# The first three weight pieces multiplied in quarters, as pairs of the first shift and scale come in

## The chip, the cores and the metric

The kernel runs on one core of one Trainium2 chip. The metric is the device time of one execution in microseconds (us). TensorE is PE in the profile, its weight loads PEld, VectorE is DVE, ScalarE is ACT, GpSimd is POOL, and SP is the engine that issues most transfers.

## What is computed

Two layers over 256 tokens of width 1024, in float32. Layer 0 mixes with a gated MLP, layer 1 with attention; each is followed by a mixture of experts (64 experts, 8 per token). Cut to the place that the change touches:

```
sh1, sc1, ... = split(silu(c) @ ada_w[0] + ada_b[0], 6)
h = rmsnorm(x, norm_mix[0]) * (1 + sc1) + sh1
z = gelu(h @ w_in + b_in)
u, v = split(z, 2)
v = layernorm(v);  sv = w_s @ v + b_s  (8 groups, chunks of 128 tokens)
x = x + g1 * ((u * sv) @ w_out)
x = x + g2 * moe(...)
```

The shift `sh1` and the scale `sc1` are 1024 values each, from a product of one row with a 1024 x 2048 part of `ada_w`.

## The kernel before

All weights come from memory in pieces of 1 MB (128 partitions x 2048 floats), called here by the tensors they are cut from: `wada` (the shifts, scales and gates, 24 pieces for a layer), `win` (16 pieces of `w_in`), `wout`, `wkva`, `wqkvo`, and three pieces for each expert. They land in a ring of 9 buffers with the tag "w" (`load`, L245); SP issues them in program order, and a piece whose buffer is still in use holds up those behind it.

A `wada` piece i gives 256 of the values. `Sum` in mode "p" (L312) multiplies it with 8 matmuls of 32x256 into a PSUM tile, ACT copies that back into the piece, and `total` (two matmuls with one column) adds up the four parts. `close` adds the bias on DVE. In mode "v" the multiplication is done on DVE, and one matmul pair does the rest. Piece 0 to 3 of layer 0 are the shift for feature tiles 0 to 7, two tiles each, and pieces 4 to 7 are the scale for the same tiles.

The way in, in the phase "pb": `wT` (the group weights) is masked on POOL; two matmuls add up its columns, 16 small ones make the bias rows `t2`; a loop over the 8 `wada` pieces multiplies each and totals it before the next is multiplied. In the second round of that loop `x` is normalised by the root of its mean square (`rstd_of`, `normed`) and transposed on PE (`transposed`) into four PSUM tiles. When all 8 totals stand, one addition and `scale_of` give shift and scale, and `feature_major_halves` writes the modulated h as two halves with fewer bits (`hT`: the rounded value, and what is left of it), for each of the 8 feature tiles an ACTIVATE on ACT, a CAST and a subtraction on DVE or, for the last three tiles, the subtraction on POOL.

The products with `w_in` follow as steps. The steps 0 to 15 are of class `Tok` (L476): a piece `win` i makes the steps 2i and 2i + 1, with 4 feature tiles each, for both token tiles: 24 matmuls of 128x256 a step (`mm3`: three products of the halves). Before its matmuls a step needs its weights as halves: `high` (a CAST on ACT, 128x1024) and `low` (a subtraction on DVE). `split` does `high` three steps ahead and `low` two steps ahead; there are 4 buffers for the halves (`scr`). Steps 16 to 31 (`Feat`) and then 16 of class `Out` follow. Between steps `tick` does the other `wada` and `wkva` pieces a few operations at a time (`BEGIN` says at which step each begins), and what has not begun by the end of the steps is done at the start of the expert phase by `rest` and `pump`.

`bvs` are four biases of 512 values spread over all partitions; the first is fetched by SP ahead of the steps, the others by ACT at the steps 2, 6 and 10. From the end of the way in, `pin` holds all engines to the program's order.

Of the kernel before, what the change touches and what calls it, by code (L numbers as in the profile page):

```python
# [8 lines left out]
F32 = mybir.dt.float32  # L9
# [4 lines left out]
ALU = mybir.AluOpType  # L14
# [16 lines left out]

LA = 3


ITEMS = [("a", i) for i in (16, 17, 18, 19, *range(8, 16), 20, 21, 22, 23)] + [("k", i) for i in range(8)]
# [142 lines left out]
def tile_model(ctx: ExitStack, tc: tile.TileContext, A: dict, out: bass.AP):  # L178
# [3 lines left out]
    class Ordered:  # L182


        def __init__(self, eng):
            self.eng = eng
# [33 lines left out]
    def h1(shape, dt=F32):  # L220
        return sb.tile(list(shape), dt, tag="h1", name=nm("h1"), bufs=5)
# [7 lines left out]
    def wk(shape=(P, 512), dt=F32):  # L229
        return ps.tile(list(shape), dt, tag="wk", name=nm("wk"), bufs=4)  # L230
# [176 lines left out]
    def pieces(x):  # L407

        return [x[:, q // 2, 512 * (q % 2):512 * (q % 2) + 512] for q in range(4)]
# [15 lines left out]
        G.tensor_tensor(r, ms, mhalf, ALU.pow)  # L425
        return r

    def normed(xs, rt, r):

        ro = pieces(rt)  # L430
        for q in (0, 2, 1, 3):
            if q < 2:
                V.tensor_scalar(ro[q], xs[q], r[:, 0:1], None, ALU.mult)
            else:
                S.activation(ro[q], xs[q], AF.Copy, scale=r[:, 1:2])

    def transposed(rt, tags=("wk",) * 4):

        o = []
        for c2 in range(KT // 2):  # L440
            pt = ps.tile([P, 2, 256], F32, tag=tags[c2], name=nm(tags[c2]), bufs=4)
            for cc in range(2):
                for tt in range(2):
                    c = 2 * c2 + cc
                    T.transpose(pt[:, cc, tt * P:(tt + 1) * P], rt[:, tt, c * P:(c + 1) * P], ident)
                o.append(pt[:, cc, :])
        return o

    def feature_major_halves(pts, mods, outs):

        for (hi, lo), (a, b) in zip(outs, mods):
            for c, pt in enumerate(pts):
                t = h1((P, 256))
                S.activation(t, pt, AF.Identity, bias=b[:, c:c + 1], scale=a[:, c:c + 1])
                V.tensor_copy(hi[:, c, :], t)
                (G if c > 4 else V).tensor_tensor(lo[:, c, :], t, hi[:, c, :], ALU.subtract)

    class Feat:

# [16 lines left out]
    class Tok:  # L476


        def __init__(self, w, kh, src, ep, prev=None, dst=None):
            self.w, self.kh, self.src, self.ep_, self.prev, self.p = w, kh, src, ep, prev, dst  # L480

        def part(self):
            return self.w[:, 4 * self.kh:4 * self.kh + 4, :]

        def mm(self):
            if self.p is None:
                self.p = self.prev.p if self.prev else [ac((P, 256)) for _ in range(2)]
            for tt in range(2):
                for k in range(4):
                    kk = 4 * self.kh + k  # L490
                    c = slice(tt * P, (tt + 1) * P)
                    mm3(self.p[tt], [self.src[0][:, kk, c], self.src[1][:, kk, c]],
                        [self.h[:, 0, k, :], self.h[:, 1, k, :]], kk == 0, kk == KT - 1)

        def ep(self):
            if self.kh:
# [649 lines left out]
    def phase(name):  # L1146
        return tc.tile_pool(name=name, bufs=1, reuse_waits="tile")


    with phase("pb") as pool:  # L1150
        lnb = wp.tile([2, 2048], F32, tag="w", name=nm("w"), bufs=9)
        nc.sync.dma_start(lnb, A["lnb"][:, 0:2048])
        lns = wp.tile([2, 1024], F32, tag="w", name=nm("w"), bufs=9)
# [1 line left out]
        hT = [pool.tile([P, KT, 256], F32R, tag="hh", name=nm("hh"), bufs=2) for _ in range(2)]  # L1155
        wT = pool.tile([P, 8, P], F32, tag="wT", name="wT")
        nc.sync.dma_start(wT, A["ws"].rearrange("s (g t) -> s g t", g=8))
        G.affine_select(wT, wT, [[0, 8], [1, P]], ALU.is_ge, 0.0, base=0, channel_multiplier=-1)
        t2 = b8((P, 16, P))


        for q in range(2):
            pr = wk((1, 512))
            T.matmul(pr, onesf[:, 0:1], wT[:, 4 * q:4 * q + 4, :].rearrange("s g t -> s (g t)"), start=True, stop=True)
            S.copy(lns[0:1, 512 * q:512 * q + 512], pr)
        for q in range(4):
            pt = wk((P, 4, P))
            for i in range(4):
                c = 4 * q + i
                g = c // 2  # L1170
                T.matmul(pt[:, i, :], lnb[:, c * P:(c + 1) * P], lns[:, g * P:(g + 1) * P], start=True, stop=True)
            S.copy(t2[:, 4 * q:4 * q + 4, :], pt)


        pa = wk((P, 16))
        for i in range(8):
            f = ada(0, i, load(A["wada"][0, i]), "p")
            if i == 1:
                nc.sync.dma_start(xt, A["x"].rearrange("(a p) d -> p a d", p=P))
            f.begin()  # L1180
            f.total(pa[:, 2 * i:2 * i + 2])
            if i == 1:
                rt = b8((P, 2, D))
                normed(pieces(xt), rt, rstd_of(pieces(xt), rt))
                pts = transposed(rt, ("acc",) * 4)


        wi = [None] * 16
        wo = [None] * 8
        first = []  # L1190

        def fetch(x):
# [8 lines left out]
            elif x[0] == "s":  # L1201
                first.append(expert(A["wsh"][0]))

        fetch(("i", 0))
        early = [high(wi[0][:, 4 * q:4 * q + 4, :], pool) for q in range(2)]
        for q in range(2):
            low(early[q], wi[0][:, 4 * q:4 * q + 4, :])
        V.tensor_tensor(adaT[0][:, 0:16], pa, pkc("adab0")[:, 0:16], ALU.add)
        scm = scale_of(adaT[0][:, 8:16], pkc("nmix0"), "scm0")
        feature_major_halves(pts, [(scm, adaT[0][:, 0:8])], [hT])  # L1210

        fetch(("i", 1))
        bvs = {}

        def fetch_bv(a, n):
            bvs[a] = s2((P, n))
            (S if pin else nc.sync).dma_start(bvs[a], A["bv"][:, a:a + n].to_broadcast([P, n]))

        fetch_bv(0, 512)
        nc.sync.dma_start(tab, A["tab"])  # L1220
        rw = router(0)
        weighing = weigh(0, rw)
        for x in QUEUE:
            fetch(x)
        pin.update(engines)

        uT = [b8() for _ in range(2)]
        v = [b8((P, 2048)) for _ in range(2)]
# [75 lines left out]
        steps[0].h, steps[1].h = early  # L1304
        steps += out_
        for k in range(2, LA):
            steps[k].h = high(steps[k].part(), pool)
        for k in range(n + 16):
            for at, x in BEGIN:
                if at == k:  # L1310
                    begin(x, lighter(k < 30))
            if k in (2, 6, 10):
# [12 lines left out]
            if 1 <= k <= n:  # L1325
                steps[k - 1].ep()
            if k % 4 == 1 and 1 < k < 18:
# [34 lines left out]
    with phase("pe") as pool:  # L1362
# [142 lines left out]
        ts = {}  # L1505
        for c in range(KT + 2):
            if c < KT:
                V.tensor_tensor(xT[c], pts[c], rb, ALU.mult)
# [139 lines left out]
```

## Time and profile before

| | us |
|---|---|
| median of 3 runs | 1416.7 (1415.97 to 1423.08) |
| the profiled execution, its own time | 1416.0 |
| its span, first to last instruction | 1414.2 |
| PE busy in the span | 1369.3 (97%) |
| DVE / ACT / POOL busy | 728.5 / 462.7 / 57.4 |

The profiled execution lasts 1.8 us longer than its span. Nearly every instruction of an engine carries the line L192 in the profile, that of the helper which records them, so groups are told apart by the names of the tiles. A float32 matmul is recorded as two, so that 8 of them stand as x16; those on halves (`scr`, `hh`) stand singly, and some records are missing. In a timeline a row is a run of equal instructions: its start, how long it lasts, the engine, out<-in, and in brackets the idle time ahead of it and what ended that. PEclk is the granted TensorE clock, 1.00 for 2.4 GHz and 0.50 for 1.2 GHz.

### The profile page before, as it was taken

The numbers are of one execution on the slowest core, as the hardware profiler recorded it, in microseconds if no ns is written. First come the engines' busy times: TensorE is split into PE (matmuls) and PEld (weight loads), VectorE is DVE, ScalarE is ACT, GpSimd is POOL, SyncE is SP. The second block draws the span as 40 slices with busy tenths as digits, with TensorE's granted clock in tenths as the row PEclk, the third lists the DMA queues.
The fourth block names the chain that finished last, engine by engine and source line by source line (L and its number), as shares of the span: only waits on it lengthen the run. The fifth ranks groups of instructions, "written<-read, shape, count | busy, mean of one in ns | idle before, by whom it ended". The sixth has DMA issues, their size and how long they took to land. (4 is left out here: it accounts for less than half of the span.)

```text
span 1414.2 us, 27956 instructions
## 1 busy us (share of the span) xinstructions
PE 1369.3 (97%) x11406; PEld 889.9 (63%) x11406; DVE 728.5 (52%) x1489; ACT 462.7 (33%) x958; POOL 57.4 (4%) x68
## 2 busy tenths in 40 slices
PE   7899999999999999999989999999999999999996
PEld 4799876745555555555548977775555555555553
DVE  0776655344444444444447866544444444444544
ACT  2544434212223222322234554422222222222222
POOL 0100002000000000000001121200000000000000
PEclk8899999999999999999999999999999999999999
DMA  9967776699999999999996867479999999999995
GB/s 371 366 271 304 281 248 248 229 366 425 425 426 426 425 426 425 423 426 426 426 416 277 317 242 268 173 277 396 410 426 425 426 426 425 426 424 425 426 426 217
DMA packets 72700, 516.66 MB, mean 365 GB/s; under 512 B 8308, under 2 KB 8436, under 8 KB 10358
## 3 DMA queue, kind: packets, MB, share of 16 engines
q1 hardware_dynamic: 72132, 514.03, 89.0%
q8 instruction: 91, 1.49, 0.4%
q10 hardware_dynamic: 436, 0.79, 0.2%
q14 instruction: 41, 0.34, 0.1%
HBM read 513.75 MB, written 1.05 MB: 364 GB/s over the span
## 5 line engine op out<-in xcount | busy, mean ns | idle before, releaser
L192 PE MATMUL wk<-w,b 128*32 128x256 f32 (+1 forms) x4928 | 406.6, 381 | 4.9 <-DMA w<-in_wexp_dram 4.9
L192 PEld LDWEIGHTS wk<-w,b 128*32 128x32 f32 (+1 forms) x4928 | 233.0, 121 | 144.2 <-DMA w<-in_wexp_dram 8.3
L192 DVE TENSOR_TENSOR s<-s,s 64x512 fp32r<-64x512 f32 x220 | 150.9, 686 | 125.3 <-ACT s L192 121.8
L192 PE MATMUL wk<-w,ht 128*32 128x512 f32 (+1 forms) x1232 | 212.5, 601 | 0.4 <-ACT ht L192 0.4
L192 DVE TENSOR_TENSOR s<-wk,g 128x512 f32<-128x512 f32 x110 | 76.1, 692 | 184.4 <-PE wk L192 184.4
L192 PE MATMUL wk<-s,b 128*128 128x256 f32 (+2 forms) x1024 | 149.6, 295 | 0.0
L192 ACT CAST s<-s 64x512 fp32r<-64x512 f32 x220 | 134.3, 611 | 15.1 <-DVE s L192 12.4
L192 PEld LDWEIGHTS wk<-s,b 128*128 128x128 f32 (+1 forms) x1024 | 124.7, 185 | 15.7 <-DVE scr L192 0.7
L192 ACT COPY ht<-wk 128x128 f32<-128x128 f32 x110 | 29.3, 266 | 314.1 <-PE wk L192 314.1
L192 PE MATMUL acc<-s,h 128*128 128x512 f32 x440 | 131.6, 420 | 0.4 <-DVE s L192 0.2
L192 ACT ACTIVATE b<-wk,adaT,sc 128x256 f32<-128x256 f32 x112 | 63.3, 565 | 180.7 <-DVE b L192 180.7
L192 DVE TENSOR_SCALAR b<-wk,sc,adaT 128x256 f32<-128x256 f32 x112 | 61.0, 544 | 100.8 <-PE wk L192 100.6
L192 ACT CAST scr<-w 128x1024 fp32r<-128x1024 f32 x80 | 83.5, 1049 | 87.1 <-PE wk L192 39.1
L192 PEld LDWEIGHTS wk<-w,ht 128*32 128x32 f32 (+1 forms) x1232 | 50.4, 120 | 94.3 <-issue 91.1
L192 PEld LDWEIGHTS acc<-s,h 128*128 128x128 f32 x440 | 74.0, 188 | 52.7 <-DVE s L192 38.1
L192 ACT ACTIVATE h<-wk 64x256 f32<-64x256 f32 (+1 forms) x114 | 43.0, 377 | 187.3 <-PE wk L192 187.3
L192 DVE TENSOR_TENSOR scr<-w,scr 128x1024 fp32r<-128x1024 f32 x80 | 99.3, 1248 | 4.8 <-ACT scr L192 4.5
L192 DVE SCALAR_TENSOR_TENSOR h<-wk,ws,h 64x256 f32<-64x256 f32 x110 | 53.9, 490 | 67.6 <-ACT h L192 66.8
L192 PEld LDWEIGHTS wk<-ident,h 64*128 64x128 f32 (+1 forms) x226 | 22.5, 137 | 92.9 <-issue 84.4
L192 PE MATMUL wk<-hh,scr 128*128 128x256 f32 x576 | 73.8, 285 | 0.0
L192 PEld LDWEIGHTS wk<-hh,scr 128*128 128x128 f32 x576 | 70.2, 191 | 3.3 <-issue 3.3
L192 DVE SCALAR_TENSOR_TENSOR w<-w,cs 128x256 f32<-128x256 f32 x119 | 58.6, 493 | 2.9
(240 smaller groups left out, 1256.3 us busy)
## 6 DMA issues: line engine op xcount, KB each, us to landing
w<-in_wexp_dram SPq DMA_DIRECT2D x384, 1024.0 KB, 15.1
w<-in_wada_dram SPq DMA_DIRECT2D x48, 1024.0 KB, 7.0
w<-in_win_dram SPq DMA_DIRECT2D x16, 1024.0 KB, 8.9
w<-in_wqkvo_dram SPq DMA_DIRECT2D x16, 1024.0 KB, 7.6
w<-in_wout_dram SPq DMA_DIRECT2D x8, 1024.0 KB, 4.9
w<-in_wkva_dram SPq DMA_DIRECT2D x8, 1024.0 KB, 4.8
w<-in_wsh_dram SPq DMA_DIRECT2D x6, 1024.0 KB, 5.6
xt<-in_x_dram SPq DMA_DIRECT2D x1, 1024.0 KB, 9.9
```

The lines of the kernel that those rows point to most:

```text
L192: r = f(*a, **k)
```

## The change

The order of the way in is new, and `pin` holds the engines to the program's order from its first line on.

- `x` is loaded ahead of the `wada` pieces, and the pieces come in pairs: `wada` 0 and 4, `win` 0, `wada` 1 and 5, `win` 1, `wada` 2 and 6, `win` 2, `wada` 3 and 7.
- `x` is transposed as it is; the root is spread along the tokens by two matmuls (`along`), copied to `rb`, and multiplied in after the transpose, by four DVE operations of 128x512 into `xn`.
- `modulated(q)` totals one pair, closes both, makes two values of the scale, and writes the halves of two feature tiles, all on ACT and DVE.
- `Tok.mm` takes the feature tiles it is to do. `first_mm(i, q)` multiplies a quarter of piece i (two feature tiles, 12 matmuls). Both token tiles of these three pieces share one PSUM tile (`joint`), so that three pieces need three.
- A list written out by hand mixes these with the multiplications of the pairs, `high` and `low`. The step loop begins at step 6, no longer at 0.
- The first two `bvs` are fetched by ACT, one behind the other, in the middle of that list. `BEGIN` starts at step 6 too, no longer at 4, so 20 of the other pieces begin within the steps, no longer 21.

```diff
-MAIN = [("i", i) for i in range(2, 16)] + [("o", i) for i in range(8)]
+MAIN = [("i", i) for i in range(PRE, 16)] + [("o", i) for i in range(8)]
...
-BEGIN = [(4 + 2 * i, x) for i, x in enumerate(ITEMS) if 4 + 2 * i < 46]
+BEGIN = [(2 * PRE + 2 * i, x) for i, x in enumerate(ITEMS) if 2 * PRE + 2 * i < 46]
...
-        pa = wk((P, 16))
-        for i in range(8):
-            f = ada(0, i, load(A["wada"][0, i]), "p")
...
-            f.begin()
-            f.total(pa[:, 2 * i:2 * i + 2])
...
+        def modulated(q):
+
+            pt = wk((P, 4))
+            for j, i in enumerate((q, 4 + q)):
+                fs[i].total(pt[:, 2 * j:2 * j + 2])
+            for j, i in enumerate((q, 4 + q)):
+                fs[i].close(pt[:, 2 * j:2 * j + 2])
+            c = slice(2 * q, 2 * q + 2)
+            V.scalar_tensor_tensor(scm[:, c], adaT[0][:, 8 + 2 * q:10 + 2 * q], 1.0, pkc("nmix0")[:, c], ALU.add, ALU.mult)
+            for k in (2 * q, 2 * q + 1):
+                t = h1((P, 256))
+                S.activation(t, pieces(xn)[q][:, 256 * (k % 2):256 * (k % 2) + 256], AF.Identity, bias=adaT[0][:, k:k + 1],
+                             scale=scm[:, k:k + 1])
+                V.tensor_copy(hT[0][:, k, :], t)
+                V.tensor_tensor(hT[1][:, k, :], t, hT[0][:, k, :], ALU.subtract)
...
+        modulated(0)
+        half(0)
+        bias_rows(3)
+        multiply(1)
+        first_mm(0, 0)
+        multiply(5)
+        modulated(1)
+        first_mm(0, 1)
+        half(2)
+        multiply(2)
+        half(1)
+        first_mm(1, 0)
+        first_mm(1, 1)
+        multiply(6)
+        modulated(2)
+        half(4)
+        half(3)
+        fetch_bv(0, 512)
+        fetch_bv(512, 512)
+        first_mm(0, 2)
+        first_mm(1, 2)
+        first_mm(2, 0)
+        multiply(3)
+        first_mm(2, 1)
+        half(5)
+        multiply(7)
+        first_mm(2, 2)
+        modulated(3)
+        k = 2 * PRE
+        half(k)
+        for i in range(PRE):
+            first_mm(i, 3)
+            if i:
+                steps[2 * i - 1].ep()
...
+        for k in range(k, n + 16):
```

The order on PE, at the first products with `w_in`. `w` are pieces, `scr` the halves of a `win` piece, `hh_106` and `hh_107` the two halves of h. Before, the totals of the last pieces (`c_76,w`) stand right ahead of them:

```order
L192 MATMUL wk_270<-w_268,cs 32x256 x8
L192 MATMUL wk_142<-c_76,w_268 128x1 x2
L192 MATMUL wk_284<-w_282,cs 32x256 x8
L192 MATMUL wk_142<-c_76,w_282 128x1 x2
L192 MATMUL acc_457<-scr_298,hh_106 128x256 x2
L192 MATMUL acc_457<-scr_298,hh_107 128x256
```

With the change (`w_111` and `w_113` are `wada` 0 and 4, `w_117` is `wada` 1, `w_104,w_102` make bias rows):

```order
L194 MATMUL wk_208<-w_113,cs 32x256 x8
L194 MATMUL wk_218<-w_104,w_102 128x128 x4
L194 MATMUL wk_332<-c_76,w_111 128x1 x2
L194 MATMUL wk_332<-c_76,w_113 128x1 x2
L194 MATMUL wk_351<-w_104,w_102 128x128 x4
L194 MATMUL wk_357<-w_117,cs 32x256 x8
L194 MATMUL acc_367<-scr_348,hh_106 128x256 x2
L194 MATMUL acc_367<-scr_348,hh_107 128x256
```

The first quarter now stands behind the totals of one pair and the multiplication of `wada` 1, and five more multiplications stand behind it.

The order on SP, at the first pieces. Before:

```order
L249 DMA w_143<-in_wada_dram 128x2048
L249 DMA w_157<-in_wada_dram 128x2048
L1179 DMA xt<-in_x_dram 128x2x1024
L249 DMA w_212<-in_wada_dram 128x2048
L249 DMA w_226<-in_wada_dram 128x2048
```

With the change:

```order
L1145 DMA xt<-in_x_dram 128x2x1024
L251 DMA w_111<-in_wada_dram 128x2048
L251 DMA w_113<-in_wada_dram 128x2048
L251 DMA w_115<-in_win_dram 128x2048
L251 DMA w_117<-in_wada_dram 128x2048
L251 DMA w_119<-in_wada_dram 128x2048
```

`x` goes ahead of two pieces, and `win` 0 is now the fourth transfer of 1 MB instead of the tenth.

The order on ACT behind the third pair (`h_109`, `h_110` are its modulated tiles, `scr_485` and `scr_554` halves of `win` 2, `w_129` and `w_131` are `wada` 3 and 7). With the change:

```order
L194 ACTIVATE h_109_477<-b_19_141,adaT_96,scm_224 128x256
L194 ACTIVATE h_110_481<-b_19_141,adaT_96,scm_224 128x256
L194 CAST scr_485<-w_127 128x1024
L194 CAST scr_488<-w_121 128x1024
L194 DMA s_113_491<-in_bv_dram 128x512
L194 DMA s_114_493<-in_bv_dram 128x512
L194 COPY w_129<-wk_532 128x256
L194 CAST scr_554<-w_127 128x1024
L194 COPY w_131<-wk_557 128x256
```

Before, no transfer stood on ACT ahead of a copy that the shift waits for. In the built program the first of the two waits until `wada` 3 has landed, the second until `win` 3 has.

## Rows read from the trace of the kernel before

**Rows 1.** The page, 40 slices of the span: granted clock and DMA share, tenths.

```profile
PEclk8899999999999999999999999999999999999999
DMA  9967776699999999999996867479999999999995
```

**Rows 2.** Busy time by stretch: stretch, length, busy us (instructions), clock, DMA share, GB/s.

```profile
13.00:26.00 13.00, 12.02 (x72) 7.39 (x75) 2.99 (x9) 4.06 (x10) 0.70 (x1) 0.50 1.01 425
...
27.00:36.00 9.00, 6.57 (x80) 3.89 (x80) 0.00 (x0) 1.86 (x5) 0.00 (x0) 1.00 0.92 351
37.00:46.00 9.00, 4.94 (x27) 3.61 (x20) 5.61 (x15) 6.27 (x12) 0.00 (x0) 0.50 1.01 425
44.00:46.00 2.00, 2.00 (x10) 2.00 (x11) 2.00 (x6) 2.00 (x5) 0.00 (x0) 0.50 1.04 430
...
60.00:200.00 140.00, 140.00 (x1151) 125.66 (x1150) 94.28 (x170) 61.15 (x101) 1.82 (x2) 1.00 0.76 282
...
240.00:245.00 5.00, 4.47 (x51) 2.34 (x51) 4.63 (x10) 3.38 (x7) 5.00 (x5) 0.66 0.36 115
...
310.00:340.00 30.00, 30.00 (x282) 16.98 (x280) 14.12 (x29) 7.63 (x17) 0.00 (x0) 1.00 1.01 423
```

**Rows 3.** Timeline of PE on the way in.

```profile
9.70 4.48 PE L192 MATMUL wk<-w,w 2*128 2x128 f32 x32
...
17.48 1.93 PE L192 MATMUL wk<-w,cs 128*32 128x256 f32 x16
...
22.37 3.25 PE L192 MATMUL acc<-ident,b 128*128 128x128 f32 x14
...
29.56 0.61 PE L192 MATMUL wk<-c,w 128*128 128x1 f32 x4 [0.48 <-ACT w L192]
30.09 1.07 PE L192 MATMUL wk<-w,cs 128*32 128x256 f32 x16
...
38.64 1.01 PE L192 MATMUL wk<-c,w 128*128 128x1 f32 x4 [0.47 <-ACT w L192]
...
43.83 5.72 PE L192 MATMUL acc<-scr,hh 128*128 128x256 f32 x34 [0.68 <-DVE scr L192]
50.58 16.20 PE L192 MATMUL acc<-scr,hh 128*128 128x256 f32 x133 [1.04 <-POOL hh L192]
66.72 1.07 PE L192 MATMUL wk<-w,cs 128*32 128x256 f32 x16
```

**Rows 4.** Timeline of all engines, from the last total to the first half of h.

```profile
39.69 0.17 DVE L192 TENSOR_TENSOR adaT<-wk,pk 128x16 f32<-128x16 f32 x1 [20.23 <-PE wk L192]
39.90 0.17 DVE L192 SCALAR_TENSOR_TENSOR scm<-adaT,pk 128x8 f32<-128x8 f32 x1
40.10 1.48 ACT L192 ACTIVATE h<-acc,adaT,scm 128x256 f32<-128x256 f32 x3 [1.51 <-DVE scm L192]
40.70 0.29 DVE L192 CAST hh<-h 128x256 fp32r<-128x256 f32 x1 [0.63 <-ACT h L192]
...
41.03 0.43 DVE L192 TENSOR_TENSOR hh<-h,hh 128x256 fp32r<-128x256 f32 x1
```

**Rows 5.** Timeline of ACT: `high` of two steps, each released by a step's end.

```profile
61.11 1.05 ACT L192 CAST scr<-w 128x1024 fp32r<-128x1024 f32 x1 [1.20 <-issue]
...
64.00 1.05 ACT L192 CAST scr<-w 128x1024 fp32r<-128x1024 f32 x1 [1.84 <-PE acc L192]
```

**Rows 6.** Groups of DVE from 60 to 66 us: `low`; busy us, mean ns of one.

```profile
L192 DVE TENSOR_TENSOR scr<-w,scr 128x1024 fp32r<-128x1024 f32 x3 | 3.7, 1219 | 0.0
```

**Rows 7.** Timeline of DVE: the first use of `x`, released by its landing.

```profile
12.91 1.29 DVE L192 BATCH_NORM_STATS2 st<-xt 128x6 f32<-128x512 f32 x2 [11.15 <-DMA xt<-in_x_dram]
```

**Rows 8.** Timeline of PE after the steps and at the start of the experts.

```profile
231.45 0.66 PE L192 MATMUL wk<-ident,t 128*128 128x128 f32 x4
...
240.88 4.48 PE L192 MATMUL wk<-w,cs 128*32 128x256 f32 x48
```

**Rows 9.** Timeline of SP's queue: the first expert pieces chosen by the routing.

```profile
242.03 19.82 SPq L249 DMA_DIRECT2D w<-in_wexp_dram  x6
```

More of the change, by code (lines that the diff above doesn't have):

```diff
@@ L445, in transposed @@
                     T.transpose(pt[:, cc, tt * P:(tt + 1) * P], rt[:, tt, c * P:(c + 1) * P], ident)
-                o.append(pt[:, cc, :])
+            o.append(pt)
         return o
[L449 to L456, printed above, removed]
     class Feat:
@@ L476, in tile_model, with __init__, mm @@
     class Tok:
-        def __init__(self, w, kh, src, ep, prev=None, dst=None):
-            self.w, self.kh, self.src, self.ep_, self.prev, self.p = w, kh, src, ep, prev, dst
+        def __init__(self, w, kh, src, ep, prev=None):
+            self.w, self.kh, self.src, self.ep_, self.prev, self.p = w, kh, src, ep, prev, None
+            self.joint = False
         def part(self):
             return self.w[:, 4 * self.kh:4 * self.kh + 4, :]
-        def mm(self):
+        def mm(self, ks=range(4)):
             if self.p is None:
@@ L488, in mm @@
             for tt in range(2):
-                for k in range(4):
+                for k in ks:
                     kk = 4 * self.kh + k
@@ L492, in mm @@
                     mm3(self.p[tt], [self.src[0][:, kk, c], self.src[1][:, kk, c]],
-                        [self.h[:, 0, k, :], self.h[:, 1, k, :]], kk == 0, kk == KT - 1)
+                        [self.h[:, 0, k, :], self.h[:, 1, k, :]], kk == 0 and not (self.joint and tt), kk == KT - 1)
         def ep(self):
@@ L1157, in tile_model, with bias_rows @@
         nc.sync.dma_start(wT, A["ws"].rearrange("s (g t) -> s g t", g=8))
+        nc.sync.dma_start(xt, A["x"].rearrange("(a p) d -> p a d", p=P))
+        wi = [None] * 16
+        wo = [None] * 8
+        wa = {}
+        for q in range(4):
+            for i in (q, 4 + q):
+                wa[i] = load(A["wada"][0, i])
+            if q < PRE:
+                wi[q] = load(A["win"][q])
         G.affine_select(wT, wT, [[0, 8], [1, P]], ALU.is_ge, 0.0, base=0, channel_multiplier=-1)
         t2 = b8((P, 16, P))
[L1162 to L1166, printed above, removed]
+        def bias_rows(q):
             pt = wk((P, 4, P))
@@ L1172, in tile_model, with multiply @@
             S.copy(t2[:, 4 * q:4 * q + 4, :], pt)
-        pa = wk((P, 16))
-        for i in range(8):
-            f = ada(0, i, load(A["wada"][0, i]), "p")
-            if i == 1:
-                nc.sync.dma_start(xt, A["x"].rearrange("(a p) d -> p a d", p=P))
-            f.begin()
-            f.total(pa[:, 2 * i:2 * i + 2])
[L1182 to L1189, printed above, removed]
+        for q in range(2):
+            pr = wk((1, 512))
+            T.matmul(pr, onesf[:, 0:1], wT[:, 4 * q:4 * q + 4, :].rearrange("s g t -> s (g t)"), start=True, stop=True)
+            S.copy(lns[0:1, 512 * q:512 * q + 512], pr)
+        xn = b8((P, 2, D))
+        r = rstd_of(pieces(xt), xn)
+        pts = transposed(xt, ("acc",) * 4)
+        fs = {}
+        def multiply(i):
+            fs[i] = ada(0, i, wa[i], "p")
+            fs[i].begin()
+        bias_rows(0)
+        multiply(0)
+        bias_rows(1)
+        pr = along([r[:, tt:tt + 1] for tt in range(2)])
+        rb = h1((P, 256))
+        S.copy(rb, pr)
+        for q in range(4):
+            V.tensor_tensor(pieces(xn)[q].rearrange("p (c t) -> p c t", c=2), pts[q], rb.unsqueeze(1).to_broadcast([P, 2, 256]),
+                            ALU.mult)
+        multiply(4)
+        bias_rows(2)
+        scm = cst.tile([P, KT], F32, name="scm0")
+        def modulated(q):
[12 more added lines that the diff above has]
+                V.tensor_tensor(hT[1][:, k, :], t, hT[0][:, k, :], ALU.subtract)
         first = []
@@ L1202, in fetch @@
                 first.append(expert(A["wsh"][0]))
[L1204 to L1212, printed above, removed]
         bvs = {}
@@ L1216, in fetch_bv @@
             bvs[a] = s2((P, n))
-            (S if pin else nc.sync).dma_start(bvs[a], A["bv"][:, a:a + n].to_broadcast([P, n]))
-        fetch_bv(0, 512)
+            S.dma_start(bvs[a], A["bv"][:, a:a + n].to_broadcast([P, n]))
+        for x in QUEUE[:4]:
+            fetch(x)
         nc.sync.dma_start(tab, A["tab"])
@@ L1222, in tile_model @@
         weighing = weigh(0, rw)
-        for x in QUEUE:
+        for x in QUEUE[4:]:
             fetch(x)
-        pin.update(engines)
         uT = [b8() for _ in range(2)]
@@ L1303, in tile_model, with half, first_mm @@
         n = len(steps)
-        steps[0].h, steps[1].h = early
         steps += out_
-        for k in range(2, LA):
+        def half(k):
             steps[k].h = high(steps[k].part(), pool)
-        for k in range(n + 16):
+            low(steps[k].h, steps[k].part())
+        def first_mm(i, q):
+            if q == 0:
+                t = ac((P, 2, 256))
+                steps[2 * i].p = [t[:, 0, :], t[:, 1, :]]
+                steps[2 * i].joint = True
+            steps[2 * i + q // 2].mm((2 * (q % 2), 2 * (q % 2) + 1))
+        modulated(0)
[32 more added lines that the diff above has]
+                steps[2 * i - 1].ep()
+        v_stats(0)
+        half(k + 1)
+        steps[k + 2].h = high(steps[k + 2].part(), pool)
+        for k in range(k, n + 16):
             for at, x in BEGIN:
@@ L1326, in tile_model @@
                 steps[k - 1].ep()
-            if k % 4 == 1 and 1 < k < 18:
+            if k % 4 == 1 and 5 < k < 18:
                 v_stats(128 * (k - 5))
```

13 lines of the change are left out of this document (4 added, 9 removed).

## The prediction

> **What bounds the kernel now.** I read the 40 slices first, then the stretches, then the timelines of PE, DVE and ACT over the first 70 us, and last the places where a shift would be taken up. The slices show transfers at nine tenths in two long parts of the span and less ahead of the first [rows 1]. In the first slices the granted clock is below full speed [rows 1].
>
> From 60 to 200 us, in the steps, PE is busy 140.00 of 140.00 us at clock 1.00 with transfers at 0.76 [rows 2]: PE is the bound there, and whatever the way in saves is carried on one for one. After the steps the routing releases the expert pieces, by SP at 242.03 [rows 9], while transfers stand at 0.36 [rows 2]; they are the bound only later, at 1.01 from 310 us on [rows 2]. So a shift of the steps moves the start of the transfer-bound part with it. What counts is **when step 6 starts**, since from there both kernels have the same work in the same order, but for which small sums lie between.
>
> Before, 168 matmuls on halves (seven steps) end where the row of multiplications at 66.72 starts [rows 3]. One step lasts 64.00 - 61.11 = 2.89 us [rows 5], so step 6 starts at 63.8; the ACT row that step 5's end releases says 64.0 [rows 5]. I take 63.9.
>
> Ahead of that the last total ends at 38.64 + 1.01 = 39.65 [rows 3], and no step has begun. The transfers were not what PE waited for at the end of that: from 27 to 36 us each round takes 2.1 us of multiply, copy and total, one behind the other (0.48 us idle ahead of a total) [rows 3].
>
> **The change, part by part.** PE's instructions in order, priced once at each of the two clock levels.
>
> *Up to the totals of the first pair.* The column sums end at 9.70 as before [rows 3]. Then 16 transposes: 14 took 25.55 - 22.37 = 3.2 at 1.2 GHz, 0.23 each, so 3.6, or by half 1.8 at 2.4 GHz. Three sets of bias rows: 16 matmuls took 4.4, so 3.3. Two multiplications: 1.93 low, 1.07 high. The spreading of the root: 0.66 high [rows 8], 1.3 low. Two totals: 1.01 low [rows 3], high 30.09 - 29.56 = 0.53 from start to start. Sum: 9.7 + 3.6 + 3.3 + 3.9 + 1.3 + 2.0 = 23.8 low, 9.7 + 1.8 + 3.3 + 2.1 + 0.7 + 1.1 = 18.7 high. I take 20, nearer to high: the clock is low from 13 us on, behind narrow bias rows [rows 2, 3], and wide transposes now stand there.
>
> *Transfers.* `x` lands at 12.9 [rows 7]; two pieces less ahead of it, at 1.05 MB by 425 GB/s = 2.47 us each [rows 2], makes 8.0. Piece n behind it then lands at 8.0 + 2.47n: `wada` 4 at 12.9, `wada` 1 at 17.8, `wada` 5 at 20.3, `wada` 6 at 27.7, `wada` 7 at 35.1, `win` 3 at 37.6, `win` 4 at 42.6. PE comes to each 2 us or more later by the times below, so no transfer binds. Buffers: the first reused ones come free with the totals at 20, when transfers are queued up to 25. If this cover went, each piece late by 2.47 us would cost that much.
>
> *The chain of a pair.* From the end of the last total (39.65) to the end of the first CAST of h (40.99) [rows 4] is 1.34, and one close more (0.17) makes **1.5 us** in which PE waits, four times. For the first pair the weights are later: two ACTIVATE, a CAST of 1.05 [rows 5] and a `low` of 1.22 [rows 6] end 3.9 after the totals, and the second matmul needs them: 23.9. Bias rows and `wada` 1 fill most of that.
>
> *From 23.9 to step 6, high.* 144 matmuls, six steps of 2.89: 17.3. Five multiplications: 5.3. Six totals: 3.2. Three waits of a pair: 4.5. Behind the third pair DVE has four operations on h and two `low` ahead of quarter (1, 2): ready 5.1 after the totals, wanted at 1.5 + 1.4, so 2.1. Sum 32.4: step 6 at **56.3**.
>
> *The same, low.* A matmul on halves then takes 0.20 (10 in 2.00 us at clock 0.50 [rows 2]): 28.8, and 9.7, 6.1, 4.5 and 1 with it, from 23.8 + 3.9: step 6 at **77.8**.
>
> *Which clock.* Before, it was 0.50 from 13 to 26 and from 37 to 46 us [rows 2]. It was up again behind transposes without a break, and it rose within the first steps (34 matmuls in 5.72 us, 0.17 each, between the two prices); it was down behind bias rows, and behind multiplications and totals with 0.5 us between them [rows 3]. After the change each of the four pairs brings such a narrow stretch with a wait, and at least 12 wide matmuls behind it. So I expect a fall and a rise for each pair. The shortest low spell I can read is 3.4 us (0.66 over 5 us [rows 2]). Part of it, about 1.5 us, lies over the wait and costs nothing: 4 x (3.4 - 1.5) / 2 = 3.8, bounds 0 and 21.5 from the two sums. Step 6 at 56.3 + 3.8 = **60.1**, a gain of 3.8 us.
>
> The rows give low spells that end as soon as wide work runs. The Trainium skill, "TensorE: Matmul & The Clock Gate", section "Loop structure matters more than you think", holds that a loop which waits for a transfer ahead of each group of matmuls lets TensorE go cold and should be turned so that matmuls follow each other; that speaks against this change. By that rule the low sum would hold, 77.8, by the rows 60.1.
>
> *Other edits.* DVE gets four operations of 128x512 in place of two, ready by 22 at the latest, and the first close comes at 20 to 24: 0 to 2 us, taken as 0. The three subtractions that POOL had go to DVE, counted above. The two bias transfers on ACT hold up its queue until `wada` 3 (32.7) and `win` 3 (37.6) have landed; ACT comes to them at about 40, so nothing, but the copy of `wada` 3 and with it the last pair stand behind them. One small sum leaves the steps (1.07 + 0.53) and joins three at the start of the experts, where 24 matmuls take 4.48 [rows 8]: saved and paid, 0. Step 6 and on need `win` 5 at about 63; it lands at about 50.
>
> **The sum:** the profiled execution of 1416.0 less 3.8 is **1412.2**. The median of the runs is 0.7 above that execution. A measurement of this kernel tells about 0.5% from no change, 7 us: the forecast is no change that can be told.
>
> **The rivals.**
>
> *The clock stays up.* If 12 to 36 wide matmuls between the waits are enough to hold 2.4 GHz, step 6 starts at 55.0 to 56.3, a gain of 7.6 to 8.9: 1407 to 1408.5, just past the bound. For it: at 27 to 36 us clock 1.00 held with only 6.57 of 9 us busy [rows 2]. Against: it then fell in the same kind of work.
>
> *The clock stays down until step 6.* One mechanism with its price: each pair's wait comes before wide work has lasted, and most matmuls take 0.20, not 0.12. From 56.3 to 77.8 the loss is 21.5; beyond 63.9, that is if over a third of it applies, the change loses, and if all does, 13.9: 1430. For it: 13 us low in one piece with PE busy 12.02 of 13 [rows 2]. Against: the first steps raised it [rows 3].
>
> [...]
>
> *The gain is taken up later*, the way in being shorter but the experts' first pieces no earlier, since one sum more stands ahead of them or a low spell falls there: 1416. Against: transfers at 0.36 there [rows 2]. The order shows that the change does what it says, so that rival falls.
>
> **How the numbers follow.** Forecast, step 6 at 57 to 63: 0.58. Clock up: 0.23. Taken up later: 0.12. Clock down: 0.07. Faster by over 0.5% is clock up and the edge of the forecast, 0.27; slower by over 0.5% is most of clock down, 0.05; the rest 0.68. The range takes the forecast's own spread and most of clock up: 1405 to 1419, leaving out clock down and the tail of the gain.
>
> **What would show it.** Step 6's start (the row of 128x256 matmuls on halves) near 60, the four waits near 1.5 us, the first quarter near 24. Falls and rises of the clock, one for each pair: none would mean the first rival, one low stretch to 60 the second. ACT's bias transfers idle ahead of them would mean the transfers bind. PE busy all of 60 to 200 us and the expert pieces as much earlier as step 6 keep the third away. Wrong would be a start of step 6 under 56 or over 64, or an end of the steps that moves by other than its start.

## The result, and the profile after

| | before | with the change |
|---|---|---|
| median of 18 runs each, us | 1416.8 (1413.2 to 1424.2) | 1411.3 (1407.6 to 1415.1) |
| profiled execution / its span | 1416.0 / 1414.2 | 1411.5 / 1409.7 |
| start of step 6 | 63.8 | 60.1 |
| end of the steps (`onesf,ident`, x16) | 221.9 | 215.7 |
| DVE / ACT / POOL busy | 728.5 / 462.7 / 57.4 | 731.4 / 462.2 / 52.5 |

The ratio is 0.9948, with a 95% interval of 0.9932 to 0.9964: 0.5% faster, just at the bound named in the prediction. The forecast for the profiled execution was 1412.2, in a range of 1405 to 1419. One execution of `e5_before_x_first` below (1426.9 us) was in a slow state, which belongs to the execution and not to the kernel, and that run's figures leave it out.

The page's 40 slices after, PEclk and DMA as in [rows 1]:

```profile
PEclk8999999999999999999999999999999999999999
DMA  9987874799999999999996867479999999999995
```

Stretches after, columns as in [rows 2]; the second three lie tightly around the low spells of the clock:

```profile
13.00:26.00 13.00, 12.16 (x103) 8.88 (x102) 5.46 (x13) 5.65 (x11) 0.70 (x1) 0.81 1.01 426
27.00:36.00 9.00, 7.52 (x55) 5.05 (x48) 2.96 (x8) 3.18 (x6) 0.00 (x0) 0.76 1.01 428
37.00:46.00 9.00, 7.17 (x52) 5.99 (x52) 4.90 (x10) 3.35 (x5) 0.00 (x0) 0.81 0.99 365
60.00:200.00 140.00, 140.00 (x1156) 124.56 (x1155) 99.22 (x182) 63.91 (x107) 1.07 (x2) 1.00 0.78 283
...
20.00:30.00 10.00, 8.19 (x58) 5.21 (x56) 2.96 (x8) 3.62 (x7) 0.00 (x0) 0.66 1.01 426
30.00:36.00 6.00, 5.49 (x35) 3.92 (x36) 2.58 (x5) 2.34 (x5) 0.00 (x0) 0.72 1.01 427
40.00:46.00 6.00, 4.17 (x21) 3.79 (x21) 4.10 (x9) 2.98 (x4) 0.00 (x0) 0.72 0.98 357
```

In the steps PE is still busy all of 140 us. A stretch of 10 us at 0.66 holds 2 x 0.34 x 10 = 6.8 us at 1.2 GHz, one of 6 us at 0.72 holds 3.4. So the way in has three low spells (stretches at 1.2 GHz) of 6.8, 3.4 and 3.4 us, where before it had two long ones [rows 2]. Read in stretches of 0.5 us, they lie at 21.1 to 28.0, 31.4 to 34.8 and 41.6 to 45.0 us; before, the clock was low from 12.8 to 26.4 and from 36.6 to 46.8.

The timeline of PE after, answering to [rows 3]:

```profile
10.52 2.13 PE L194 MATMUL acc<-ident,xt 128*128 128x128 f32 x16
...
18.47 1.05 PE L194 MATMUL wk<-c,w 128*128 128x1 f32 x8
...
23.36 2.72 PE L194 MATMUL acc<-scr,hh 128*128 128x256 f32 x11 [0.68 <-DVE scr L194]
...
30.51 2.98 PE L194 MATMUL acc<-scr,hh 128*128 128x256 f32 x12 [1.48 <-DVE hh L194]
...
41.84 3.20 PE L194 MATMUL acc<-scr,hh 128*128 128x256 f32 x13 [1.54 <-DVE hh L194]
45.34 2.89 PE L194 MATMUL acc<-scr,hh 128*128 128x256 f32 x23 [0.29 <-DVE scr L194]
...
53.29 0.95 PE L194 MATMUL wk<-c,w 128*128 128x1 f32 x8
55.71 13.09 PE L194 MATMUL acc<-scr,hh 128*128 128x256 f32 x108 [1.47 <-DVE hh L194]
68.73 1.07 PE L194 MATMUL wk<-w,cs 128*32 128x256 f32 x16
```

The 108 matmuls are the last quarters and steps 6 to 8, so step 6 starts at 68.73 - 3 x 2.89 = 60.1. The first quarter's second matmul is at 23.4, and h is waited for 1.48, 1.54 and 1.47 us. The first of these waits, 29.0 to 30.5, lies at clock 1.00, and so does nearly all of the second, 40.3 to 41.8: the clock falls as the wait ends or just behind it, and then the quarter runs low.

`x` on DVE (before: [rows 7]), and ACT around its two bias transfers, which here wait for nothing:

```profile
8.33 1.29 DVE L194 BATCH_NORM_STATS2 st<-xt 128x6 f32<-128x512 f32 x2 [6.57 <-DMA xt<-in_x_dram]
```

```profile
40.87 0.60 ACT L194 ACTIVATE h<-b,adaT,scm 128x256 f32<-128x256 f32 x1 [1.21 <-DVE scm L194]
40.97 0.36 ACTq L194 DMA_DIRECT2D s<-in_bv_dram  x1
```

PE at the end of the steps and at the start of the experts, after and then before (more in [rows 8]):

```profile
215.72 2.03 PE L194 MATMUL wk<-onesf,ident 128*128 128x128 f32 x16
...
234.67 3.66 PE L194 MATMUL wk<-w,cs 128*32 128x256 f32 x64
238.26 5.45 PE L194 MATMUL wk<-b,w 128*128 128x256 f32 x24
...
246.95 1.50 PE L194 MATMUL wk<-c,w 128*128 128x1 f32 x12 [0.46 <-ACT GT L194]
...
249.52 7.13 PE L194 MATMUL wk<-b,w 128*128 128x256 f32 x24
256.31 4.18 PE L194 MATMUL wk<-s,b 128*128 128x256 f32 x32
```

```profile
221.93 2.03 PE L192 MATMUL wk<-onesf,ident 128*128 128x128 f32 x16
...
253.98 1.05 PE L192 MATMUL wk<-c,w 128*128 128x1 f32 x8 [0.46 <-ACT GT L192]
...
261.14 4.18 PE L192 MATMUL wk<-s,b 128*128 128x256 f32 x32
```

The steps end 6.2 us earlier and the 64 matmuls (48 before) start 6.2 us earlier, at 234.67 against 240.88. Then a low spell falls into a row of 24 matmuls: 7.13 us, where the same form takes 5.45 at 238.26. The kernel before has a spell here too: its 48 multiplications take 4.48 us at a clock of 0.66 [rows 2, 8], where three quarters of the 3.66 are 2.7. The two spells cost 1.7 us each and cancel. What costs the change is the sum that moved here: 16 more multiplications, 0.9 us, and a totals row of 1.50 us, not 1.05. So behind the spells the lead is 4.8 us (256.31 against 261.14), and the span ends 4.5 us earlier.

SP's chosen expert pieces up to 330 us, after and then before (behind the six of [rows 9]), and the stretch around their start after:

```profile
244.58 81.75 SPq L251 DMA_DIRECT2D w<-in_wexp_dram  x29
```

```profile
273.88 50.13 SPq L249 DMA_DIRECT2D w<-in_wexp_dram  x21
```

```profile
240.00:245.00 5.00, 5.00 (x27) 4.14 (x26) 2.22 (x7) 0.00 (x0) 0.25 (x1) 1.00 0.00 0
245.00:250.00 5.00, 4.07 (x26) 3.38 (x26) 0.66 (x4) 2.03 (x3) 0.00 (x0) 0.98 0.87 269
```

They start 2.5 us later than before, not earlier, but by 330 us 29 have followed in one run, where before six came first and 21 more from 273.88.

### The profile page after: what moved, and what is told of

Same layout as the page of the kernel before. It is cut to its first block, busy times and chain, and to the rows that moved or that the text cites. A ratio compares the mean times of both kernels' runs of the same rounds, so it can differ in the third digit from the quotient of the medians.

```text
span 1409.7 us, 27967 instructions
## 1 busy us (share of the span) xinstructions
PE 1367.9 (97%) x11410; PEld 889.4 (63%) x11410; DVE 731.4 (52%) x1504; ACT 462.2 (33%) x957; POOL 52.5 (4%) x65
## 3 DMA queue, kind: packets, MB, share of 16 engines
HBM read 513.75 MB, written 1.05 MB: 365 GB/s over the span
## 5 line engine op out<-in xcount | busy, mean ns | idle before, releaser
L194 PEld LDWEIGHTS acc<-s,h 128*128 128x128 f32 x440 | 74.0, 188 | 52.7 <-DVE s L194 38.0
L194 PEld LDWEIGHTS wk<-ident,h 64*128 64x128 f32 (+1 forms) x226 | 22.5, 137 | 92.9 <-issue 84.3
```

The costliest lines, as they stand in the source:

```text
L194: r = f(*a, **k)
```

## Experiments

Step 6's start is read from the profile as above: the multiplication behind steps 6 to 8, less 3 x 2.89 us, so that waits within these steps are counted in. It comes from one profile each, and has a scatter of its own: ahead of the first pair's totals all kernels below but e5 and e1 have the change's order on PE, and these totals start between 17.55 us (e4) and 19.56 us (e9), in the change at 18.47. So a difference of under 2 us in step 6 is not put down to an edit by itself. The medians are of 4 to 12 executions (the change: 18). Each ratio is to the kernel before, timed on the same chip; its medians there were 1416.8 to 1419.0 us, so the ratios compare better than the medians.

| run | step 6 at | median, us | ratio (interval) |
|---|---|---|---|
| the change | 60.1 | 1411.3 | 0.9948 (0.9932 to 0.9964) |
| e5_before_x_first | 64.4 | 1416.2 | 0.9968 (0.9939 to 0.9997) |
| e1_x_late | 65.4 | 1417.5 | 0.9993 (0.9973 to 1.0013) |
| e6_no_quarters | 58.9 | 1411.5 | 0.9946 (0.9930 to 0.9962) |
| e9_no_quarters_bias_sp | 54.6 | 1408.5 | 0.9937 (0.9925 to 0.9949) |
| e8_h_at_end | 62.7 | 1414.5 | 0.9966 (0.9950 to 0.9983) |
| e3_filler | 59.4 | 1409.8 | 0.9930 (0.9908 to 0.9953) |
| e2_totals_ahead | 53.9 | 1401.3 | 0.9860 (0.9835 to 0.9885) |
| e7_bias_by_sp | 47.9 | 1400.9 | 0.9862 (0.9837 to 0.9887) |
| e4_bias_later | 61.4 | 1415.3 | 0.9979 (0.9960 to 0.9998) |
| e10_change_bias_sp | 61.9 | 1414.9 | 0.9972 (0.9954 to 0.9989) |
| e7_again | 49.6 | 1399.0 | 0.9880 (0.9862 to 0.9898) |
| e2_again | 48.2 | 1401.8 | 0.9887 (0.9870 to 0.9903) |

### Where the gain comes from

**The early `x` alone**, in the kernel before:

```diff
+        nc.sync.dma_start(xt, A["x"].rearrange("(a p) d -> p a d", p=P))
...
-            if i == 1:
-                nc.sync.dma_start(xt, A["x"].rearrange("(a p) d -> p a d", p=P))
```

> The kernel before, with nothing changed but the load of x, which goes ahead of the wada pieces. Theory (before, the chain behind the last total was bound by the pieces, one multiplied, copied and totalled after the other, and x was not waited for at the end): the root, the normalisation and the transposes come 3 to 5 us earlier, the pieces one transfer of 2.5 us later, step 6 at 62 to 66 instead of 63.9, time 1414 to 1418. Rival (the early x is the gain of the change): step 6 at 60, time 1412.

Step 6 at 67.33 - 2.89 = 64.4 (there the multiplication stands behind step 6), 1416.2 us: as the theory said. The last total comes at 39.25, against 38.64 before, so it was not `x` that bound it; the pieces come one transfer later.

**`x` late**, in the change:

```diff
-        nc.sync.dma_start(xt, A["x"].rearrange("(a p) d -> p a d", p=P))
...
                 wa[i] = load(A["wada"][0, i])
+                if i == 4:
+                    nc.sync.dma_start(xt, A["x"].rearrange("(a p) d -> p a d", p=P))
```

> The change, with the load of x put behind the first pair of wada pieces. Theory (PE comes to the transposes of x at 10.5 us and everything behind them is in order; x then lands at about 13): all that follows is 2 to 3 us later, step 6 at 62 to 63.5, time 1413 to 1415. Rival (there is slack between the first pair and the later ones that takes it up): step 6 at 60 to 61, time 1411 to 1412.

It cost twice what the theory said: step 6 at 65.4, all of the gain. Two rows of PE on its way in show where:

```profile
12.82 3.32 PE L194 MATMUL acc<-ident,xt 128*128 128x128 f32 x16 [2.75 <-DMA xt<-in_x_dram]
...
20.50 1.94 PE L194 MATMUL wk<-w,cs 128*32 128x256 f32 x16
```

The transposes start 2.3 us later, as forecast, and they take 3.32 us, not 2.13; the profile gives a clock of 1.00 for them, so why is open. Behind them the clock is low from 19.1 to 22.5 us, and a multiplication takes 1.94 us, not 1.07. The totals of the first pair end 5.0 us later, and that stays. So by the start of step 6 the early `x` is worth nothing by itself and 5 us in the new order. (By its ratio e5 is a little faster than before, in an interval that ends at 0.9997; its profile shows no reason on the way in.)

**The quarters taken out**, that is all `first_mm` of the first six tiles behind the last pair:

```diff
         multiply(1)
-        first_mm(0, 0)
         multiply(5)
         modulated(1)
-        first_mm(0, 1)
...
+        modulated(3)
+        first_mm(0, 0)
+        first_mm(0, 1)
...
```

> The loads, pairs and roots of the change, but none of the quarters ahead of the last pair: all 144 matmuls of the first three pieces stand behind the totals of the fourth pair. Theory (what brings the gain is that h is there earlier and that PE never waits for long; the quarters only fill time in which PE else waits for weights): the last totals come at 37 to 40 us, since wada 7 lands at 35, the 144 matmuls follow in 17.3 us with a wait of 1.5 and one low spell ahead of them, step 6 at 57.5 to 61, time 1408 to 1413. Rival (the quarters, multiplied under the transfers of the later pairs, are the gain): they are 108 matmuls later, of which at most the idle time is won back, step 6 at 66 to 71, time 1417 to 1422.

The time is that of the change, and step 6 starts no later (58.9), although no quarter is multiplied ahead of 41 us. PE and ACT at the last pair:

```profile
39.44 1.87 PE L194 MATMUL wk<-c,w 128*128 128x1 f32 x8 [1.55 <-ACT w L194]
41.16 26.49 PE L194 MATMUL acc<-scr,hh 128*128 128x256 f32 x216
```

```profile
38.63 0.33 ACTq L194 DMA_DIRECT2D s<-in_bv_dram  x1
39.01 0.65 ACT L194 COPY w<-wk 128x256 f32<-128x256 f32 x2 [4.04 <-DMA w<-in_win_dram]
```

PE goes on at 41.16 without a break, since h of three pairs stands ready. And here ACT does stand behind a bias transfer, 4.04 us, until `win` 3 has landed: the stall that the prediction excluded for the change because ACT comes later there.

**The same with the bias fetched by SP**, right behind the loads of the pairs:

```diff
             if q < PRE:
                 wi[q] = load(A["win"][q])
+        bvs = {}
+        for a in (0, 512):
+            bvs[a] = s2((P, 512))
+            nc.sync.dma_start(bvs[a], A["bv"][:, a:a + 512].to_broadcast([P, 512]))
...
-        fetch_bv(0, 512)
-        fetch_bv(512, 512)
```

> The kernel without quarters ahead (e6), with the first two bias transfers by SP as in e7: in e6 ACT stood 4.0 us behind the second of them until win 3 had landed, and the last totals waited 1.55 us for ACT's copy. Theory (that was 1.5 to 2 us on the path, so what pairs alone give is more than e6 showed, and the quarters of the change cost it): the last totals start 1 to 1.6 us earlier, step 6 at 56.5 to 58 against 58.9 in e6 and 60.1 in the change, time 1408 to 1411. Rival (the bias by SP puts 0.5 MB ahead of wada 3 and wada 7, 1.2 us at 425 GB/s, and takes it back): step 6 at 58.5 to 59.5, time 1411 to 1412.5.

```profile
37.52 1.16 PE L194 MATMUL wk<-c,w 128*128 128x1 f32 x8
38.54 24.75 PE L194 MATMUL acc<-scr,hh 128*128 128x256 f32 x216
63.22 1.07 PE L194 MATMUL wk<-w,cs 128*32 128x256 f32 x16
```

Wide work starts 2.6 us earlier than in e6 and runs at the high clock from the start (24.75 us against 26.49), more than was expected. Step 6 is at 54.6, 5.5 us ahead of the change. The times of these two can't be told apart, since the intervals overlap. The fitting partner is e10 below, the change with the same bias by SP, timed on the same chip: 0.9937 without quarters against 0.9972 with them, in intervals that do not meet (up to 0.9949, from 0.9954), and step 6 at 54.6 against 61.9. So there the quarters, in the order that the change gives them, cost more than they bring.

**h at the end**: e6, but the scale, the ACTIVATEs and the halves of h for all pairs behind the last total.

```diff
+        def finish(q):
+
             c = slice(2 * q, 2 * q + 2)
             V.scalar_tensor_tensor(scm[:, c], ...
...
         modulated(3)
+        for q in range(4):
+            finish(q)
```

> The kernel without quarters ahead (e6), with the totals still taken pair by pair, but the scale, the ACTIVATEs and the halves of h made for all four pairs only behind the last total. Theory (what gains 4 to 5 us over the kernel before is that three quarters of h stand ready when the last totals end, so that PE goes on at once): PE then idles 2 to 4 us behind the last totals and starts its wide work at the low clock, step 6 starts at 62 to 65 instead of 58.9, time 1414 to 1418. Rival (the gain is in the multiplication of a pair back to back, the transposes of the raw x, or the order of the loads): step 6 starts at 61 or earlier, time 1411 to 1413.

```profile
42.98 28.44 PE L194 MATMUL acc<-scr,hh 128*128 128x256 f32 x216 [1.35 <-DVE hh L194]
71.35 1.07 PE L194 MATMUL wk<-w,cs 128*32 128x256 f32 x16
```

PE waits 1.35 us, less than expected, and the 216 matmuls take 28.44 us against 26.49, at a clock that is low for longer. Step 6 is 3.8 us later than in e6, which is most of what e6 gains over before (4.9). So by the profiles most of the gain is that h is made pair by pair while the pieces land; the times point the same way (0.9966 against 0.9946), but their intervals overlap.

### What the change leaves

**Filler** on PE in the three waits:

```diff
                 fs[i].total(pt[:, 2 * j:2 * j + 2])
+            if q:
+                warm(10)
```

> The change, with ten wide matmuls whose result nobody reads put on PE behind the totals of the second, third and fourth pair, where PE else waits about 1.5 us for h. Theory (the low spells at 31.3 and 41.5 us follow the narrow work and the wait behind it, and cost 1 to 2 us each): with PE kept in wide work there the granted clock is 1.00 from 30 us on, and step 6 starts at 56.5 to 59 instead of 60.1, time 1407.5 to 1410.5. Rival (the chain through ACT and DVE alone sets the pace, the clock costs nothing here): the clock is 1.00 too, and step 6 stays at 60 to 61, time 1411 to 1412.5. If the filler costs more than the wait it fills, step 6 is later than 61.

Step 6 at 59.4, between theory and rival, and the time can't be told from that of the change. PE around the filler of the second and third pair:

```profile
29.72 2.48 PE L194 MATMUL wk<-onesf,ident 128*128 128x128 f32 x20
31.95 1.62 PE L194 MATMUL acc<-scr,hh 128*128 128x256 f32 x12
...
41.73 1.89 PE L194 MATMUL acc<-scr,hh 128*128 128x256 f32 x13
44.67 2.88 PE L194 MATMUL acc<-scr,hh 128*128 128x256 f32 x23 [1.05 <-DVE scr L194]
```

The clock is up: 12 matmuls in 1.62 us, not 2.98. From the second pair's totals to the third's that gives 1.35 us (9.88 us against 11.23); half of it does not show in step 6, since this execution came to the first pair's totals 0.7 us later. Behind the third pair PE waits 1.05 us for `low`, not 0.29, and nothing more is won. The clock was worth something only where no wait stood behind it.

**Totals ahead** of the quarters that they used to follow, so that PE has wide work while h is made:

```diff
-        first_mm(0, 0)
         multiply(5)
         modulated(1)
-        first_mm(0, 1)
         half(2)
+        first_mm(0, 0)
         multiply(2)
...
+        modulated(3)
+        fetch_bv(0, 512)
+        fetch_bv(512, 512)
+        first_mm(0, 2)
+        first_mm(1, 2)
+        first_mm(2, 2)
```

> The change, with the totals of the next pair put ahead of the quarter products that were multiplied before them, so that PE has 12 to 24 wide matmuls to do while ACT and DVE turn the totals into h. Theory (the waits behind the totals, 1.5 us each, and the low spells that come with them are what is left to win on the way in): the rows idle ahead of a quarter fall from about 1.5 us to under 0.5, fewer low spells than the three of the change (6.8, 3.4, 3.4 us), step 6 starts at 48 to 55 instead of 60.1, time 1400 to 1406. Rival (the transfers of the pieces bind as soon as PE comes to them earlier): the idle time moves to the rows ahead of the multiplications, ended by a DMA, and step 6 starts no earlier than 57, time 1408 or more.

1401.3 us, 0.986 of before, and the waits for h are gone. One stretch and two rows of PE:

```profile
13.00:26.00 13.00, 13.00 (x122) 9.72 (x121) 5.83 (x15) 6.17 (x13) 0.70 (x1) 0.86 1.02 428
```

```profile
42.29 9.79 PE L194 MATMUL acc<-scr,hh 128*128 128x256 f32 x84
53.52 1.65 PE L194 MATMUL acc<-scr,hh 128*128 128x256 f32 x12 [1.44 <-DVE b L194]
```

The profile shows no break of PE up to 52 us, so no transfer binds. The wait in step 6 is for step 1's epilogue on DVE, and that waits for the bias: moved behind the last pair it is issued at 42.9 and lands at 52.7.

**Totals ahead, bias by SP** (e2 with the diff of e9):

> The kernel with the totals ahead (e2), with the first two bias transfers fetched by SP right behind the loads of the pairs, not by ACT behind the last pair. Theory (in e2 the bias is issued at 42.9 us and lands at 52.7, so that step 1's epilogue comes late and PE, which needs its PSUM tile, idles 1.44 us in step 6 and 1.3 us more behind it): the bias is there by 38, these idle times go, and the first three steps from step 6 on end 2 to 3.5 us earlier than in e2, where they end at 62.6; time 1397.5 to 1400. Rival (the pieces win 3 and win 4 or the chain of the halves bind as well): they end at 61.5 or later, time 1400.5 to 1403.

```profile
40.02 16.59 PE L194 MATMUL acc<-scr,hh 128*128 128x256 f32 x144
```

In the profile the wait is gone and steps 6 to 8 end at 56.54, 6.0 us earlier. That is more than the 2 to 3.5 expected, but 1.3 us of it are there at the first pair's totals (17.78 against 19.08), ahead of any edit. The median stays (1400.9), within the rival's range. The lead over e2 is still 5.8 us at the end of the steps and 4.8 us at 860 us; then two stretches of 10 us, e2's first, e7's behind:

```profile
870.00:880.00 10.00, 10.00 (x82) 7.40 (x81) 6.00 (x13) 0.94 (x3) 0.00 (x0) 1.00 0.39 164
...
900.00:910.00 10.00, 7.67 (x43) 6.40 (x43) 8.33 (x50) 7.12 (x13) 4.95 (x4) 1.00 0.29 95
```

```profile
870.00:880.00 10.00, 10.00 (x69) 8.02 (x68) 2.61 (x8) 1.29 (x5) 0.00 (x0) 0.83 0.08 14
...
900.00:910.00 10.00, 8.85 (x34) 7.05 (x34) 5.22 (x20) 3.84 (x7) 4.95 (x4) 0.66 0.62 237
```

The low spells, 3.4 and 6.8 us, lie in e7's execution alone, and behind them the lead is 0.3 us.

**The late bias alone**, in the change: both `fetch_bv` behind `modulated(3)`.

> The change, with the two bias transfers on ACT behind the last pair, as e2 has them. Theory (a bias issued there lands 8 to 10 us later, too late for the epilogue of step 1): PE idles 3 to 7 us in step 6, which is the cost of the place of these transfers by itself, time 1414 to 1418. Rival (in e2 something else held step 6, and ACT is freed by 0.8 us ahead of the third pair's halves): no idle time in step 6, time 1410.5 to 1412.

```profile
61.23 1.64 PE L194 MATMUL acc<-scr,hh 128*128 128x256 f32 x12 [0.46 <-DVE b L194]
```

The wait is there, with 0.41 and 0.88 us more for the halves behind it. From the last quarters to the end of step 8 it takes 15.6 us, not 13.0: 2.6 us, less than the 3 to 7 expected.

**The bias by SP alone**, in the change (the diff of e9):

> The change with the first two bias transfers by SP, its order else unchanged. Theory (in the change these transfers cost nothing, since ACT comes to them after the pieces have landed and the bias is there in time; what e7 gains over e2 is the late bias alone): step 6 at 59.5 to 60.5, time 1410.5 to 1412.5. Rival (the place of the bias on ACT costs the change too): step 6 at 59 or earlier.

Step 6 at 61.9 and 1414.9 us: neither. The last totals are 0.8 us later than in the change, 0.55 of it already at the first pair's, and the 108 matmuls behind them take 14.10 us, not 13.09, with the clock at 0.87 from 46 to 60 us, where the change has 1.00. No engine waits for the bias. Its interval overlaps that of the change; whether the 3 us are the transfers' or the clock's is left open.

**e7 and e2 once more**, unchanged:

> e7 once more, unchanged, for a second profile and more times. On the way in e7 was 6.0 us ahead of e2, and still 4.8 us ahead at 860 us; from 870 to 910 us its profile has low spells (clock 0.83 and 0.66 in slices of 10 us) that e2's has not, and its lead is 0.3 us behind them. Theory (what the head gains is given back to low spells whose places change with the alignment of the kernel's work): the second profile shows them in the same places if they belong to the kernel, in others if they belong to the execution; the median stays at 1399 to 1402 in either case. Rival (the transfers take the lead back): the lead is lost where the transfers are at full share, with the clock at 1.00.

> e2 once more, unchanged, beside e7 on the same chip. Theory (e7 keeps part of the 6 us): e2 is 0 to 4 us slower than e7 in the medians, 1399 to 1404; its second profile has low spells between 720 and 920 us that the first had not, if they belong to the execution. Rival (the 6 us are lost in every execution): the medians are within 1 us of each other.

e7's second profile has no low spell from 870 to 880 us, and 0.95 and 0.88 from 890 to 910: other places. e2's has the pattern of e7's first, 0.83 and 0.66, and up to there it also runs like it: a row of 20 matmuls of `onesf,ident` in layer 1 starts at 728.85 us in the one and at 728.73 in the other. So these spells belong to the execution, not to the kernel; the two executions that share them also share their timing. The second profile also corrects the first: here the bias is issued 2.3 us earlier and lands in 6.6 us, not 9.8 (DVE, e2 and then e2 again), and PE waits for nothing.

```profile
52.71 1.42 DVE L194 TENSOR_TENSOR b<-acc,s 128x256 f32<-128x256 f32 x4 [6.50 <-DMA s<-in_bv_dram]
```

```profile
47.24 1.42 DVE L194 TENSOR_TENSOR b<-acc,s 128x256 f32<-128x256 f32 x4 [3.30 <-DMA s<-in_bv_dram]
```

So what e7 showed over e2 was in part an execution of e2 in which the bias came late. The two can't be told apart by their times (0.9862 and 0.9880 against 0.9860 and 0.9887). Both are faster than the change, by 0.6 to 0.9% in the ratios, about 10 us, and are the fastest kernels here.

## Why the prediction was right, step by step

- **Up to the first pair's totals**: 20 forecast, 19.5 measured. `x` 8.0 forecast, in use at 8.33.
- **The chain of a pair**: 1.5 us, three times: 1.48, 1.54, 1.47. The first quarter's second matmul: 23.9 against 23.4.
- **The wait for `low` behind the third pair**: 2.1 us forecast, 0.29 measured. The quarter ahead of it ran at the low clock, 13 matmuls in 3.20 us, so DVE had time; at the high clock (e3) the wait is 1.05.
- **The clock**: a fall and a rise for each of four pairs, 4 x 3.4 = 13.6 us low in all. Measured: three spells, the first twice as long, 13.6 us in all, none at the fourth pair. Their cost was mis-sized: the high sum with the measured waits is 56.3 - 1.8 - 0.5 = 54.0, and step 6 came at 60.1, so the spells cost 6.1 us, not 3.8. Behind 23.4 us the clock was low for 11.4 us, and half of that, 5.7, is nearly all of it. The 1.5 us of each spell that were taken off as lying over the wait were hardly there: the second and third spell begin behind a wait or as it ends, over busy matmuls. This and the `low` wait cancelled: the 60.1 is right to 0.1 us by luck, by two errors of 2 us.
- **Bias transfers at nothing**: right for the change; e6 shows the stall that was excluded, 4.04 us of ACT, once ACT comes to them earlier.
- **Saved and paid, 0**: the steps end 6.2 us earlier, 3.7 of it from their start and 2.5 from within. The sum that left them is 1.7 of the 2.5 by its rows in the two profiles (forecast 1.6); the rest is spread over rows that both kernels have. At the experts the sum costs 1.4. That makes 3.7 + 2.5 - 1.4 = 4.8, and the span gains 4.5. The end of the steps moved by other than their start, which the prediction named as a sign of being wrong; its own sum, with 1.6 leaving the steps, already implied such a difference.
- **The expert pieces**, said to come as much earlier as step 6: wrong for the first of them (244.58 against 242.03), with transfers at 0.00 just ahead. It cost nothing that the span shows, since from 245 to 260 us they run at 0.87 and more.
- **The rivals**: the clock neither stayed up nor down. That the gain is taken up later is true of the sum that moved, 1.4 us; the low spell at 249.52 that the rival feared has its match in the kernel before.
- **The time**: the profiled executions differ by 4.5 us, the medians by 5.5, forecast 3.8. With 18 executions each that can be told from no change (the interval ends at 0.9964), which the prediction held for too little to tell.

The prediction took from its rows that a spell ends as soon as wide work runs. That was misread: from 44 to 46 us before, PE does wide work for 2.00 us at 0.50 [rows 2], and here each quarter behind a spell's start ran low nearly whole (2.72, 2.98 and 3.20 us for 11, 12 and 13 matmuls). The first spell ended only in the next pair's totals, at 28.0.

The Trainium skill, "TensorE: Matmul & The Clock Gate", section "Loop structure matters more than you think", sets matmuls that follow one another against a long wait for a transfer between every matmul, 8 us in its example, behind which TensorE runs cold. No run here has waits of that length, so the low sum of 77.8 that the prediction drew from it applied the page to another case. With waits of 1.5 us the clock came back after each spell, and step 6 started at 60.1. What the page recommends holds here: e2, whose matmuls follow one another, is about 10 us faster than the change.

What the prediction did not ask is what the quarters bring. Without them (e6, e9) the way in is no slower. They pay once the totals stand ahead of them: step 6 at 48 to 54 (e2, e7) instead of 54.6 to 58.9, with ratios of 0.9860 to 0.9887 instead of 0.9937 and 0.9946. As the change has them, each quarter from the second pair on waits for its own pair's h.

Over all runs the way in carries through to the time nearly one for one: from step 6 at 63.8 to 48 or 50 it is 14 to 16 us, and the medians differ by 16 to 19. One kernel's executions differ by 5 to 13 us, though (e5's by 20), and two kernels whose step 6 is 1 to 6 us apart (e6 and the change, e7 and e2) can have the same median.

## What to carry to other kernels

When weights come in pieces that a later product needs, make that product's input piece by piece; but ahead of multiplying early, put the small work that releases the next input, so that the wide work covers its chain. Price a wait with the clock behind it, and look at what comes next: a faster stretch that runs into the next wait wins nothing. A short profile gain at the start of a long kernel needs a second profile of the same kernel before it is put down to an edit.

## What was not expected

- TensorE's clock fell with PE busy without a break: 0.86 in 13 us with 13.00 of 13.00 us busy (e2), behind bias rows, multiplications and totals. A wait is not needed for it; in e7's second execution PE shows no idle time from 10 us to step 6, and the clock is low from 21.7 to 28.5 all the same.
- Two executions of one kernel differed by 5.6 us at the end of step 8 (62.56 and 56.91), and by 0.5 us in their time (1402.7 and 1402.2): low spells from 870 to 910 us, in the second alone, took up most of the difference.
- A bias of 256 KB fetched by ACT behind SP's pieces took 6.6 and 9.8 us to land (e2's two executions); by its size, at the 425 GB/s of [rows 2], the estimate is 0.6.
